# A third buffer for the raw weight chunks of a fused decoder layer

## The chip, the cores and the metric

The kernel runs on one core of a Trainium2 chip. The metric is the device time of one execution in microseconds, taken as the median of several runs. The engines are named as in the profile: PE is the matrix engine, PEld its weight loads, DVE the vector engine, ACT the scalar engine, POOL the general engine GpSimd, and SP the engine that issues most of the DMA transfers.

## The reference

One layer of a decoder for 256 tokens with 1024 features, all in float32: a gated sum of block attention (16 heads of 64; with 256 tokens there is one block, so it is plain causal attention) and a gated linear recurrence (8 heads), then cross-attention to 256 memory tokens (4 heads of 256), then a SwiGLU feed-forward part with 2816 hidden features.

```python
xn = rmsnorm(h, norm_mix_g[l])
q_a, k_a, v_a, q_b, f_b, i_b, og_b, g_a, g_b = split_cols(xn @ w_in[l])
y_a = moba_attention(q_a, k_a, v_a, positions) @ w_br_attn[l]
y_b = hgrn2(q_b, f_b, i_b, og_b, lb_all[l], hgrn_norm_g[l]) @ w_br_hgrn[l]
merged = jax.nn.sigmoid(g_a) * y_a + jax.nn.sigmoid(g_b) * y_b
h = h + merged @ w_out[l]
h = h + memory_cross_attention(rmsnorm(h, norm_x_g[l]), rmsnorm(mem, norm_mem_g[l]),
                               wq_x[l], wkv_x[l], wo_x[l])
hn = rmsnorm(h, norm_ffn_g[l])
gu = hn @ w_ffn_in[l]
h = h + (jax.nn.silu(gu[..., :FFN_HIDDEN]) * gu[..., FFN_HIDDEN:]) @ w_ffn_out[l]
return rmsnorm(h, final_norm_g)
```

## The kernel before, in words

All weights are laid out in main memory as chunks of 1 MB (128 partitions x 2048 floats), in the order in which they are used. Chunks 0 to 63 belong to the part ahead of the feed-forward part: 0 to 35 are the nine input projections, 36 to 47 the two branch projections and the output projection `w_out`, 48 to 59 the cross-attention's keys, values and queries, 60 to 63 its output projection. Each matrix product is made from three products of reduced-precision operands: every number is split into a rounded part `hi` and a remainder `lo`.

So each chunk takes three steps. SP issues its load into a buffer `raw` (L204; the first chunks in pieces at L202 and L208). ACT copies it in two halves to `hi` (L210), and DVE subtracts to get `lo` (L214); for chunks 9 to 41 POOL takes a part of the subtraction. Then PE multiplies. This is the function `prep`; `nxt` calls it so that chunk i+2 is prepared in the program when chunk i is about to be used. `raw` has two buffers in turn (chunk 1 alone has another place), `hi` and `lo` three each. A load waits until the chunk that had the buffer before is converted; a conversion waits until PE is done with the chunk that had the `hi` buffer three chunks before. The chunks 62 and 63 have places of their own for `hi` and `lo` (called `hix` and `lox` in the profile), where the cross-attention's keys and queries were.

The order of PE's instructions is the program's. In the part ahead of the feed-forward part the order on ACT, DVE and SP, and on POOL but for the opening, is made by a planner: it lays out the instructions by its own costs, program order giving the priority, and each engine then runs its list in order, waiting where an operand isn't there. In the feed-forward part all orders are the program's.

Small work runs between the chunks: `tick`, called after each chunk, advances generators for the recurrence (`hgrn`), the causal attention (`attention`, two heads at a time in `duo`: scores L805, maxima L812, exponentials L817, scaling L821, transposes L829, value products L838) and the cross-attention (`scores`: maxima L1046, xmx L1048, exponentials L1050, scaling L1054, transposes L1060). For the fourth cross-attention head the scores come after chunk 58, the transposes after chunk 59, and then `pv` multiplies by the values `vxh` and `vxl` (L319, L320 from `ev_vx`).

Other memory that matters: `H` holds the input by token (x, 1 MB, L540), loaded in the opening; its squares give the norm r_x (L560), from which the first gates `fth` (L512) are made. H is next used at the output projection, where the residual is added (`add_h`). `QQ` (place B6, 16 KB per partition) holds the recurrence's query variants for two groups of four heads; the same place holds later `oal`, `qxl`, `lox` and then the feed-forward's `hids`. QK (place P0) holds the recurrence's queries and keys. In the background ACT and POOL issue transfers from main memory to main memory that make sums of feed-forward weights (`sum`, L228, L232, L234).

Of the kernel before, what the change touches and what calls it, by code (L numbers as in the profile page):

```python
# [11 lines left out]
F32R = mybir.dt.float32r  # L12
I32 = mybir.dt.int32
AF = mybir.ActivationFunctionType
# [15 lines left out]
TOKENS = ((0, 1), (1, 2), (2, 4), (4, 8))  # L30
WARM = 15
PIECES = (4, 2, 2)

D1, D2, D3, D4 = 6434.0, -0.01824188232421875, -3.5660341382026672e-06, 2.549093241608853e-10
C1, C2, C3 = 6.28125, 0.0019354820251464844, -1.748455600074497e-07
# [98 lines left out]
def build(tc, A, out):  # L134
    nc = tc.nc
    V, SC, G, PE, SY = nc.vector, nc.scalar, nc.gpsimd, nc.tensor, nc.sync
    with ExitStack() as ctx:
# [11 lines left out]
        def big(tag, name, shape=(128, 8, 256), dt=F32):  # L149
            return bp.tile(list(shape), dt, name=name, tag=tag)  # L150
# [21 lines left out]
        ifq, posi = gv[:, 56:88], gv[:, 88:90].bitcast(I32)  # L172
        nhalf = cp.tile([128, 4], F32, name="nhalf")
        ident = cst[:, C_ID:C_ID + 128]
        H = big("B0", "H", (128, 2, 1024))
        ones = cp.tile([128, 1], F32, name="ones")
        V.memset(nhalf, -0.5)
        V.memset(ones, 1.0)
# [5 lines left out]
        def prep(tags=None, raw=None):  # L184
            i = made[0]
            made[0] += 1
            first = i < 2
            if raw is None:
                raw = wr.tile([128, 2048], F32, name="raw", tag="raw")
            assert i in HEAD  # L190
            if tags is None:
                hi = wh.tile([128, 2048], F32R, name="hi", tag="hi")
                lo = wl.tile([128, 2048], F32R, name="lo", tag="lo")
            else:
                hi = big(tags[0], "hix", (128, 2048), F32R)
                lo = big(tags[1], "lox", (128, 2048), F32R)
            pieces = 4 if first else 2
            n = 2048 // pieces
            sent = PIECES[i] if i < len(PIECES) else 1
            for c in range(sent if 0 < i < len(PIECES) else 0):  # L200
                a = slice(c * 2048 // sent, (c + 1) * 2048 // sent)
                SY.dma_start(raw[:, a], piece(A["w"][i], a))  # L202
            if sent == 1:
                SY.dma_start(raw, A["w"][i])  # L204
            for c in range(pieces):
                a = slice(c * n, (c + 1) * n)
                if i == 0:
                    SY.dma_start(raw[:, a], piece(A["w"][i], a))  # L208
                    yield
                SC.activation(hi[:, a], raw[:, a], AF.Copy)  # L210
                cut = (c + 1) * n - (POOL_COLS // pieces if i in SHARED else 0)
                for eng, b in ((V, slice(c * n, cut)), (G, slice(cut, (c + 1) * n))):
                    if b.start < b.stop:
                        eng.tensor_tensor(lo[:, b], raw[:, b], hi[:, b].bitcast(F32), op=ALU.subtract)  # L214
            ready[i] = (hi, lo)
# [85 lines left out]
        def gemm_t(X, evict, between=()):  # L301
            between = list(between)
            pss = [mm.tile([128, 512], F32, name="pst", tag="mm") for _ in range(2)]
            for kh in range(2):
                w = by_k(nxt(), 4)
                for t in range(2):
                    t_part(pss[t], w, X, t, kh)
                    if between:
                        between.pop(0)()
                    if kh == 1:  # L310
                        evict(t, pss[t])
                tick()
# [9 lines left out]
        def rstd_of(ssq, name, n=2, mult=1.0 / D, eps=EPS):  # L322
            v = small("v_", [n])
            V.tensor_scalar(v, ssq, mult, eps, op0=ALU.mult, op1=ALU.add)
            r = cp.tile([128, n], F32, name="r_" + name)
            G.tensor_tensor(r, v, nhalf[:, :n], op=ALU.pow)
            return r
# [142 lines left out]


        fT = big("B4", "fT", (128, 16, 128))
        QK = big("P0", "QK", (128, 2, 16, 128))
        QP, KS = QK[:, 0], QK[:, 1]
        QQ = big("B6", "QQ", (128, 16, 256))

        gate_a = cp.tile([128, 8], F32, name="gate_a")
        gate_b = cp.tile([128, 8], F32, name="gate_b")
# [38 lines left out]
        def ev_q(c):  # L517
            th = {}

            def use(h0, bk):  # L520
                a = slice(2 * h0, 2 * h0 + 4)
                q4 = bk.rearrange(v4, a=2)
                V.tensor_tensor(QP[:, a], q4, fT[:, a], op=ALU.mult)
                SC.activation(QQ[:, a].rearrange("p a (w j) -> p a w j", w=4)[:, :, 0:4:3],
                              q4.rearrange("p a (j w) -> p a w j", w=2), AF.Copy)

            def ev(t, ps):
                th[t] = t2("qth")
                SC.activation(th[t], ps, AF.Silu, scale=r_x[:, t:t + 1])
                if t == 1:  # L530
                    turned(th, c, use)
            return ev
# [4 lines left out]
        run(prep())  # L537
        SY.dma_start(cst, A["cst"])
        run(prep())
        SY.dma_start(H, A["xtok"])  # L540
        SY.dma_start(lm, A["lm"])
        pss = [[mm.tile([128, 512], F32, name="psg", tag="mm") for _ in range(2)] for _ in range(2)]
        for i in range(9):
            if i < 8:
                c, k = i // 4, i % 4
                for z in (Xh, Xl):
                    for t in range(2):
                        PE.matmul(pss[c][t], z[:, k, t * 128:(t + 1) * 128], ws[c][0][:, k],
                                  start=z is Xh and k == 0, stop=False)
# [4 lines left out]
        w = by_k(nxt(), 4)  # L554
        for t in range(2):
            t_part(pss[0][t], w, X, t, 1)
        ssqx = small("ssqx", [2])
        junk = big("P1", "junk", (128, 2, 1024))
        for t in range(2):
            SC.activation(junk[:, t], H[:, t], AF.Square, accum_out=ssqx[:, t:t + 1])  # L560
        r_x = rstd_of(ssqx, "x")
        next(rt)
        next(rt)
        r_half = cp.tile([128, 2], F32, name="r_half")
# [5 lines left out]
        w = by_k(nxt(), 4)  # L570
# [33 lines left out]
        def level_one(g, bs):  # L604
            for b in bs:
                a0 = 8 * g + 2 * b
                ps = bank("l1", (128, 2, 64))
                for j in range(2):
                    PE.matmul(ps[:, j], KS[:, a0 + j], QQ[:, a0 + j, 0:64], start=True, stop=True)
                V.tensor_tensor(by_parity(a0, 0), ps, bc(ident2[:, :, 0], 2, 1), op=ALU.mult)  # L610

        def widen(g, L, parts="qkt"):
# [23 lines left out]
        def pair_queries(g, L):  # L636
            ga = slice(8 * g, 8 * g + 8)
            n = 32 // L
            mv = [QQ[:, ga, 64 * i:64 * i + 64] for i in range(3)]
            SC.activation(mv[0].rearrange("p a (i j) -> p a i j", j=L), blocks(QP[:, ga], L)[1], AF.Copy)  # L640
            widen(g, L, "qt")
            wide = blocks(QP[:, ga], 2 * L)[1]
            SC.activation(mv[1].rearrange("p a (i j) -> p a i j", j=2 * L), wide, AF.Copy)
            near = tview(L, g).rearrange("p a (i w) -> p a i w", w=4)[:, :, :, 1]
            V.tensor_tensor(mv[2].rearrange("p a (i j) -> p a i j", j=2 * L), wide,
                            near.unsqueeze(3).to_broadcast([128, 8, n, 2 * L]), op=ALU.mult)

        def pair_levels(g, L, bs):
            for b in bs:
                a0 = 8 * g + 2 * b  # L650
                n = 256 if L == 2 else 192
                ps = bank("lp", (128, 2, n))
                for j in range(2):
                    PE.matmul(ps[:, j], KS[:, a0 + j], QQ[:, a0 + j, 0:n], start=True, stop=True)  # L654
                if L == 2:
                    V.tensor_tensor(by_parity(a0, 1), ps[:, :, 192:256], bc(two_rows, 2, 1), op=ALU.mult)
                for i in range(3):
                    M = L if i == 0 else 2 * L
                    li = (1 if L == 2 else 4) + i
                    mask = lm[:, 64 * li:64 * li + 64].rearrange("p (i j) -> p i j", j=M)  # L660
                    V.copy_predicated(blocks(at3[:, a0:a0 + 2], M)[1], bc(mask, 2, 1),
                                      ps[:, :, 64 * i:64 * i + 64].rearrange("p a (i j) -> p a i j", j=M))
# [219 lines left out]
        def ev_g(dst, c):  # L882
            def ev(t, ps):
                SC.activation(dst[:, t, c * 512:(c + 1) * 512], ps, AF.Tanh, scale=r_half[:, t:t + 1])
            return ev
# [23 lines left out]
        turns = []  # L909
        for c in range(2):  # L910
            gemm_t(X, ev_g(tbt, c))
        tat = big("B7", "tat", (128, 2, 1024))
        for c in range(2):
            gemm_t(X, ev_g(tat, c))
# [149 lines left out]
        for c in range(4):  # L1064
            gemm_f(H1, ev_sum(qxh, qxl, c))
            g = scores(c)
# [123 lines left out]
        raws += spare + [big("B12", "raw", (128, 2048))]  # L1190
        fetch(4)
        fetch(5)
        hids = big("B6", "hids", (128, 4, 2, 2, 256), F32R)
        Sh = big("P1", "Sh", (128, 2, 4, 4, 128), F32R)
        ts = {}

# [40 lines left out]
        def turn_hid(o):  # L1237
            bk = four[1].rearrange("p (a b) -> p a b", a=2)
            for t in range(2):
                u = hm.pop((o, t))  # L1240
                for j in range(2):
                    PE.transpose(bk[:, j, t * 128:(t + 1) * 128], u[:, j * 128:(j + 1) * 128], ident)
            hd = hids[:, o % 4]
            hid[o] = hd

            def post():
                split(bk, hd[:, 0], hd[:, 1])
            return post
# [37 lines left out]
        for k, u in enumerate(FFN[:-2]):  # L1286
            if u[0] == "I":
                ahead(k)
                w = use(k)
# [170 lines left out]
```

## Time and profile before

| | |
|---|---|
| median of 3 runs | 624.73 us (623.67 to 625.43) |
| the profiled execution, total | 626.06 us |
| its span, first to last instruction | 624.3 us |
| PE busy | 606.2 us (97%) |
| DVE, ACT, POOL busy | 450.5, 369.2, 210.2 us |
| DMA | 154.70 MB, mean 248 GB/s |
| mean granted clock of PE | 0.991 |

A row of the view of groups or of the timeline names the source line, the engine, the operation, and what it writes and reads ("raw<-w" is a load of a weight chunk). In the timeline the first two columns are start and duration in microseconds; a bracket at the end gives the idle time of the engine before this instruction and what ended it. In the view of waits each row gives who waited, for whom, the total in microseconds, how often, and the longest. In the view by stretches each row has the busy time and the number of instructions of each engine, then the granted clock of PE, the share of the 16 DMA engines that was busy, and GB/s.

### The profile page before, as it was taken

The page shows a single profiled execution, that of the slowest core. Times are in us where ns is not written, and L with a number is a line of the kernel's source. Part 1 is how long each engine was busy: PE and PEld are TensorE (multiplying, and loading weights), DVE is VectorE, ACT ScalarE, POOL GpSimd, SP SyncE. Part 2 cuts the span into 40 slices and gives each one's busy share as a digit, 9 for nine tenths or more (in the row PEclk, how much of TensorE's full clock was granted, in tenths as well). Part 3 has the DMA queues.
Part 4 walks back from the last instruction along what each step waited for, and adds up shares of the span by engine and source line. Part 5 has one row for each costly group of instructions (what it writes and reads, how often), then busy time and mean ns, then how long its engine had stood idle before and what let it go on. Part 6 is the DMA issues. An engine that isn't in the chain of part 4 may idle for free.

```text
span 624.3 us, 8396 instructions
## 1 busy us (share of the span) xinstructions
PE 606.2 (97%) x3075; PEld 503.1 (81%) x3075; DVE 450.5 (72%) x729; ACT 369.2 (59%) x583; POOL 210.2 (34%) x202
## 2 busy tenths in 40 slices
PE   8999999999999999999999999959999999999995
PEld 7888888888877887778888888858888888888884
DVE  7556678987776775747966557746789878787863
ACT  7775454334267666745546557555477767676752
POOL 3887844665464565343302433100000000000003
PEclk9999999999999999999999999979999999999998
DMA  9775898636875656797798887765699989896601
GB/s 342 289 276 210 266 318 262 228 140 198 270 208 204 257 152 198 276 322 265 228 286 240 304 283 239 229 256 203 264 289 356 307 333 288 319 319 227 195 1 67
DMA packets 21689, 154.70 MB, mean 248 GB/s; under 512 B 2720, under 2 KB 3360, under 8 KB 5280
## 3 DMA queue, kind: packets, MB, share of 16 engines
q1 hardware_dynamic: 17568, 116.63, 49.4%
q0 software_dynamic: 2880, 20.97, 17.4%
q10 hardware_dynamic: 1200, 16.57, 7.0%
q8 instruction: 24, 0.39, 0.2%
q14 instruction: 17, 0.14, 0.1%
HBM read 153.11 MB, written 32.51 MB: 297 GB/s over the span
## 4 chain that ended last, share of the span: by engine, by line
PE 78%; DMA 9%; DVE 8%; ACT 2%; issue 1%; POOL 0%; POOLq 0%; ACTq 0%; DVEq 0%; SPq 0%
PE pst L275 10%; PE pst L277 10%; PE pst L276 10%; DMA raw<-w 8%; PE bk L275 6%; PE bk L277 6%; PE bk L276 6%; DVE lo L214 4%; PE psf L290 3%; PE acc L275 3%; PE acc L277 3%; PE acc L276 3%; PE lp L654 2%; PE psf L291 2%; ACT hi L210 1%
## 5 line engine op out<-in xcount | busy, mean ns | idle before, releaser
L214 DVE TENSOR_TENSOR lo<-raw,hi 128x576 fp32r<-128x576 f32 (+2 forms) x128 | 143.7, 1137 | 68.4 <-ACT hi L210 67.4
L210 ACT ACTIVATE hi<-raw 128x1024 fp32r<-128x1024 f32 (+1 forms) x128 | 128.0, 1028 | 109.1 <-DMA raw<-w 53.6
L214 POOL TENSOR_TENSOR lo<-raw,hi 128x448 fp32r<-128x448 f32 x66 | 98.0, 1504 | 79.2 <-ACT hi L210 72.9
L275 PE MATMUL pst<-hi,Xh 128*128 128x512 f32 x256 | 103.2, 403 | 0.0
L277 PE MATMUL pst<-hi,Xl 128*128 128x512 f32 x256 | 99.9, 390 | 0.0
L276 PE MATMUL pst<-lo,Xh 128*128 128x512 f32 x256 | 99.7, 390 | 0.0
L1165 DVE TENSOR_TENSOR lo<-raw,hi 128x1024 fp32r<-128x1024 f32 x56 | 65.9, 1218 | 13.0 <-ACT hi L1164 12.8
L1164 ACT ACTIVATE hi<-raw 128x1024 fp32r<-128x1024 f32 x56 | 56.2, 1053 | 19.8 <-issue 10.5
L277 PEld LDWEIGHTS pst<-hi,Xl 128*128 128x128 f32 x256 | 48.0, 188 | 10.3
L275 PEld LDWEIGHTS pst<-hi,Xh 128*128 128x128 f32 x256 | 48.1, 188 | 10.0 <-issue 0.7
L276 PEld LDWEIGHTS pst<-lo,Xh 128*128 128x128 f32 x256 | 48.2, 188 | 9.2
L1147 POOL DMA_DIRECT2D raw<-w x5 | 4.5, 891 | 119.2 <-DVE lo L1165 29.7
L275 PE MATMUL acc<-hi,hids 128*128 128x512 f32 x64 | 25.1, 392 | 0.0
L277 PE MATMUL acc<-hi,hids 128*128 128x512 f32 x64 | 24.9, 390 | 0.0
L276 PE MATMUL acc<-lo,hids 128*128 128x512 f32 x64 | 24.9, 389 | 0.0
L275 PE MATMUL bk<-hi,Sh 128*128 128x512 f32 x60 | 23.7, 396 | 0.0
L275 PE MATMUL bk<-hi,h2h 128*128 128x512 f32 x60 | 23.7, 394 | 0.0
L277 PE MATMUL bk<-hi,h2l 128*128 128x512 f32 x60 | 23.4, 390 | 0.0
L277 PE MATMUL bk<-hi,Sh 128*128 128x512 f32 x60 | 23.4, 390 | 0.0
L276 PE MATMUL bk<-lo,h2h 128*128 128x512 f32 x60 | 23.4, 389 | 0.0
L276 PE MATMUL bk<-lo,Sh 128*128 128x512 f32 x60 | 23.3, 389 | 0.0
L290 PE MATMUL psf<-H,hi 128*128 128x512 f32 x64 | 22.8, 400 | 0.0
(388 smaller groups left out, 1446.8 us busy)
## 6 DMA issues: line engine op xcount, KB each, us to landing
raw<-w SPq DMA_DIRECT2D x78, 1024.0 KB, 6.4
sum<-w POOLq DMA_DIRECT2D x15, 1024.0 KB, 9.8
raw<-sum SPq DMA_DIRECT2D x13, 1024.0 KB, 6.9
raws<-w SPq DMA_DIRECT2D x11, 1024.0 KB, 6.7
raw<-w POOLq DMA_DIRECT2D x5, 1024.0 KB, 8.7
raw<-w SPq DMA_DIRECT2D x4, 512.0 KB, 6.1
raws<-sum SPq DMA_DIRECT2D x2, 1024.0 KB, 6.3
raw<-w SPq DMA_DIRECT2D x4, 256.0 KB, 4.5
```

The lines of the kernel that those rows point to most:

```text
L210: SC.activation(hi[:, a], raw[:, a], AF.Copy)
L214: eng.tensor_tensor(lo[:, b], raw[:, b], hi[:, b].bitcast(F32), op=ALU.subtract)
L275: PE.matmul(ps, xh, h, start=first, stop=False, skip_group_check=more)
L276: PE.matmul(ps, xh, l, start=False, stop=False, skip_group_check=more)
L277: PE.matmul(ps, xl, h, start=False, stop=last, skip_group_check=more)
L290: PE.matmul(ps, w[0][:, k, a], X2[:, :, k], start=k == 0, stop=False)
L291: PE.matmul(ps[:, 0], w[1][:, k, a], X2[:, 0, k], start=False, stop=k == 7)
L654: PE.matmul(ps[:, j], KS[:, a0 + j], QQ[:, a0 + j, 0:n], start=True, stop=True)
L1147: G.dma_start(raw_of[k], A["w"][AT_CHUNK["I", PAIRS[g][0], 1]], accum_op=ALU.add)
L1164: SC.activation(hi[:, a], raw[:, a], AF.Copy)
L1165: V.tensor_tensor(lo[:, a], raw[:, a], hi[:, a].bitcast(F32), op=ALU.subtract)
```

## The change

Every third raw chunk (2, 5, 8, ...) of the part ahead of the feed-forward part no longer takes one of the two buffers in turn, but a place of its own: up to chunk 29 the place B0, where H was, and from chunk 32 on the place B6b. B6b is the second half of what was B6: QQ becomes two tiles of half the size, one for each group of heads, and `hids` becomes two tiles likewise. B0 is free at the start since the token-major input is first loaded to the place P0 as `xtok`, where its squares are written over it (before, they went to a tile `junk` at P1), and QK takes P0 after it. The input is loaded a second time to H, at B0, in the program after the chunks of the gate g_b. The number of the other instructions is as it was.

```diff
@@ prep
             first = i < 2
-            if raw is None:
+            if raw is None and i % 3 == 2:
+                raw = big("B0" if i < THIRD else "B6b", "raw", (128, 2048))
+            elif raw is None:
                 raw = wr.tile([128, 2048], F32, name="raw", tag="raw")
...
-        QK = big("P0", "QK", (128, 2, 16, 128))
-        QP, KS = QK[:, 0], QK[:, 1]
-        QQ = big("B6", "QQ", (128, 16, 256))
+        xtok = big("P0", "xtok", (128, 2, 1024))
+        QQ = [big(tag, "QQ", (128, 8, 256)) for tag in ("B6", "B6b")]
...
-        SY.dma_start(H, A["xtok"])
+        SY.dma_start(xtok, A["xtok"])
...
-        junk = big("P1", "junk", (128, 2, 1024))
         for t in range(2):
-            SC.activation(junk[:, t], H[:, t], AF.Square, accum_out=ssqx[:, t:t + 1])
+            SC.activation(xtok[:, t], xtok[:, t], AF.Square, accum_out=ssqx[:, t:t + 1])
         r_x = rstd_of(ssqx, "x")
+        QK = big("P0", "QK", (128, 2, 16, 128))
+        QP, KS = QK[:, 0], QK[:, 1]
...
         for c in range(2):
             gemm_t(X, ev_g(tbt, c))
+        H = big("B0", "H", (128, 2, 1024))
+        SY.dma_start(H, A["xtok"])
...
-        hids = big("B6", "hids", (128, 4, 2, 2, 256), F32R)
+        hids = [big(tag, "hids", (128, 2, 2, 2, 256), F32R) for tag in ("B6", "B6b")]
```

THIRD is 32. The rest of the diff only renames the places where QQ and hids are read and written.

More of the change, by code (lines that the diff above doesn't have):

```diff
@@ L32 @@
 PIECES = (4, 2, 2)
+THIRD = 32
 D1, D2, D3, D4 = 6434.0, -0.01824188232421875, -3.5660341382026672e-06, 2.549093241608853e-10
@@ L174, in build @@
         ident = cst[:, C_ID:C_ID + 128]
-        H = big("B0", "H", (128, 2, 1024))
         ones = cp.tile([128, 1], F32, name="ones")
@@ L523, in use @@
                 V.tensor_tensor(QP[:, a], q4, fT[:, a], op=ALU.mult)
-                SC.activation(QQ[:, a].rearrange("p a (w j) -> p a w j", w=4)[:, :, 0:4:3],
+                qa = slice(a.start % 8, a.start % 8 + 4)
+                SC.activation(QQ[a.start // 8][:, qa].rearrange("p a (w j) -> p a w j", w=4)[:, :, 0:4:3],
                               q4.rearrange("p a (j w) -> p a w j", w=2), AF.Copy)
@@ L608, in level_one @@
                 for j in range(2):
-                    PE.matmul(ps[:, j], KS[:, a0 + j], QQ[:, a0 + j, 0:64], start=True, stop=True)
+                    PE.matmul(ps[:, j], KS[:, a0 + j], QQ[g][:, a0 + j - 8 * g, 0:64], start=True, stop=True)
                 V.tensor_tensor(by_parity(a0, 0), ps, bc(ident2[:, :, 0], 2, 1), op=ALU.mult)
@@ L638, in pair_queries @@
             n = 32 // L
-            mv = [QQ[:, ga, 64 * i:64 * i + 64] for i in range(3)]
+            mv = [QQ[g][:, :, 64 * i:64 * i + 64] for i in range(3)]
             SC.activation(mv[0].rearrange("p a (i j) -> p a i j", j=L), blocks(QP[:, ga], L)[1], AF.Copy)
@@ L653, in pair_levels @@
                 for j in range(2):
-                    PE.matmul(ps[:, j], KS[:, a0 + j], QQ[:, a0 + j, 0:n], start=True, stop=True)
+                    PE.matmul(ps[:, j], KS[:, a0 + j], QQ[g][:, a0 + j - 8 * g, 0:n], start=True, stop=True)
                 if L == 2:
@@ L1242, in turn_hid @@
                     PE.transpose(bk[:, j, t * 128:(t + 1) * 128], u[:, j * 128:(j + 1) * 128], ident)
-            hd = hids[:, o % 4]
+            hd = hids[o % 4 // 2][:, o % 2]
             hid[o] = hd
```

## The prediction

> **What bounds the kernel now.** I read the page first: TensorE (PE) is busy nearly all the span, so only its idle time, and any time at a lower granted clock, can be won. Then the waits of PE alone say where it idles.
>
> ```profile
> span 624.3 us, 8396 instructions
> PE 606.2 (97%) x3075; PEld 503.1 (81%) x3075; DVE 450.5 (72%) x729; ACT 369.2 (59%) x583; POOL 210.2 (34%) x202
> PE xT L1060 <- DVE xp L1054: 6.3, 1, 6.3
> PE aT L829 <- DVE ap L821: 1.7, 3, 0.9
> PE warm L365 <- DVE still L362: 1.6, 1, 1.6
> PE xs L277 <- POOL qxl L1017: 0.8, 1, 0.8
> PE as L805 <- ACT pT L831: 0.5, 1, 0.5
> PE psg L548 <- ACT hi L210: 0.4, 1, 0.4
> PE mT L903 <- POOL tat L898: 0.3, 1, 0.3
> ```
>
> PE idles 624.3 - 606.2 = 18.1 us. The seven waits hold 11.6 of it; the other 6.5 belong to no wait of PE's, most of it the tail after the last matmul, which the change doesn't touch. One wait, 6.3 us before the transposes of the fourth cross-attention head (L1060), is over half of what could move. The ACT and DVE queues around it:
>
> ```profile
> 403.13 0.57 ACT L316 ACTIVATE ph<-xT 128x512 fp32r<-128x512 f32 x1
> 409.79 2.00 ACT L210 ACTIVATE hix<-raw 128x1024 fp32r<-128x1024 f32 x2 [6.08 <-DMA raw<-w]
> 411.69 0.58 ACT L1050 ACTIVATE xp<-xp,xmx,r 128x256 f32<-128x256 f32 x1
> 404.75 0.15 DVE L1048 SCALAR_TENSOR_TENSOR xmx<-xmx,r 128x2 f32<-128x2 f32 x1
> 404.81 1.22 DVE L214 TENSOR_TENSOR lo<-raw,hi 128x1024 fp32r<-128x1024 f32 x1
> 413.07 1.20 DVE L214 TENSOR_TENSOR lox<-raw,hix 128x1024 fp32r<-128x1024 f32 x1
> 414.19 0.61 DVE L1054 TENSOR_SCALAR xp<-xp,xsum 128x256 f32<-128x256 f32 x2
> 414.72 1.40 DVE L320 SCALAR_TENSOR_TENSOR vxl<-pst,r_m,vxh 128x512 fp32r<-128x512 f32 x2
> ```
>
> The head's maxima are ready at 404.90, but its exponentials (L1050) start at 411.69: they stand in ACT's queue behind the conversion of chunk 62 (hix), which waits 6.08 us for that chunk's load. PE waits for weights that it doesn't need until much later. The pause also costs clock afterwards (columns: stretch, us, busy time of PE, PEld, DVE, ACT, POOL, granted clock, DMA share, GB/s):
>
> ```profile
> 394.50:400.70 6.20, 6.20 (x32) 5.24 (x32) 4.30 (x9) 3.75 (x8) 2.92 (x3) 1.00 0.42 149
> 408.10:414.60 6.50, 0.17 (x2) 0.01 (x1) 2.84 (x5) 4.32 (x8) 0.00 (x0) 0.78 0.46 166
> 414.60:418.60 4.00, 4.00 (x19) 3.92 (x20) 2.21 (x4) 0.84 (x2) 0.00 (x0) 0.51 0.76 276
> 418.60:422.60 4.00, 4.00 (x35) 4.00 (x35) 3.36 (x4) 3.98 (x5) 0.00 (x0) 1.00 0.59 248
> 160.00:190.00 30.00, 28.80 (x162) 23.19 (x161) 20.66 (x42) 16.56 (x29) 14.20 (x10) 1.00 0.87 280
> ```
>
> At clock 0.51 PE starts 19 matmuls in 4 us, at full clock 35 of the same kind. Four of the 19 are half as wide, so they would have taken (15 + 2) / 35 x 4 = 1.9 us plus about 0.2 for the switch: some 1.9 us lost.
>
> **The change, part by part.**
>
> *The third buffer.* Chunks 57 to 63 now use the two old slots (57, 58, 60, 61, 63) and a third one (59, 62). So chunk i waits for the conversion of chunk i-3, no longer i-2: its load can be issued when that of chunk i-1 was issued before. The 61 loads of L204 are chunks 3 to 63 in order. The issues of chunks 61 and 62, and from the DMA view the times to landing of chunks 59, 60 and 62:
>
> ```profile
> L204 SPq DMA_DIRECT2D raw<-w x61: 327/328/882, 9.7 to 406.1; - x61
> 391.28 0.33 SPq L204 DMA_DIRECT2D raw<-w  x1
> 399.91 0.33 SPq L204 DMA_DIRECT2D raw<-w  x1
> raw<-w SPq DMA_DIRECT2D x1, 1024.0 KB, 4.7
> raw<-w SPq DMA_DIRECT2D x1, 1024.0 KB, 10.7
> raw<-w SPq DMA_DIRECT2D x1, 1024.0 KB, 9.8
> ```
>
> Chunk 62 moves from 399.91 to 391.28. With the longest landing here, 10.7 us, it lands at 402.0, against 409.7; DMA had room, with a share of 0.42 in 394.5 to 400.7. ACT is free for hix when ph ends, 403.70: so hix runs 6.09 us earlier, to 405.7, and the exponentials follow to 406.8. What is late next is DVE: its lo of chunk 61 ends at 406.03, then two lox of 1.2 with a short reciprocal between, and xp starts near 408.5; the transposes came 0.41 us after xp's start (414.19 to 414.60), so at 408.9. PE is free at 414.60 - 6.33 = 408.27: 0.6 us of idle stay. Right after, DVE's two vxl take 1.40 us from about 409.05, to 410.4, while the first value product reaches the matmul that reads the second of them after four transposes and five matmuls, near 409.9: another 0.5 us. Waits of this length cost no clock: the waits of 160 to 190 (0.93 and 0.27 us, below) left it at 1.00. The step gives 6.3 - 0.6 - 0.5 + 1.9 = 7.1 us; bounds 0 (ACT still stands) and 8.2.
>
> The Trainium skill, "TensorE: Matmul & The Clock Gate", section "Why this matters for your kernels", says that a pause of more than about 3 us between bursts puts TensorE at half rate. The 0.51 after 6.33 us agrees. By that rule a remainder of up to 3 us would still save the whole clock loss; by scaling the row, one of 3 us would keep some 0.9 of it.
>
> *The same step in the attention stage.* Two of its three PE waits trace to a load:
>
> ```profile
> 179.40 2.01 ACT L210 ACTIVATE hi<-raw 128x1024 fp32r<-128x1024 f32 x2 [1.64 <-DMA raw<-w]
> 184.38 0.61 PE L829 MATMUL aT<-cst,ap 128*128 128x128 f32 x3 [0.93 <-DVE ap L821]
> 185.26 0.61 PE L829 MATMUL aT<-cst,ap 128*128 128x128 f32 x3 [0.27 <-DVE ap L821]
> 187.83 1.06 ACT L210 ACTIVATE hi<-raw 128x1024 fp32r<-128x1024 f32 x1 [3.24 <-DMA raw<-w]
> 194.18 0.33 PE L829 MATMUL aT<-cst,ap 128*128 128x128 f32 x1 [0.49 <-DVE ap L821]
> 162.50 0.33 SPq L204 DMA_DIRECT2D raw<-w  x1
> 174.48 0.33 SPq L204 DMA_DIRECT2D raw<-w  x1
> ```
>
> The load for the conversion at 179.40 (chunk 28) moves from 174.48 to 162.50; the one for 187.83 moves likewise. With ACT no longer standing 1.64 and 3.24 us, I take 1.4 of the 1.69 us (0.3 stays, DVE's own lo stands between); bounds 0 and 1.7.
>
> *The other five waits.* warm and psg (1.6 and 0.4 us) lie in the opening, before a third buffer matters. xs (0.8) waits for a POOL result that stood behind a conversion in ACT's queue, and that one for PE's release of a hi buffer, which stays; as and mT (0.5, 0.3) wait for evictions. 0, bounds 0 and 1.6 gained.
>
> *Loads that are queued earlier at the start.* Chunk 3 no longer waits, and chunk 4 waits for chunk 0, so it may go ahead of the token-major input in SP's queue, where it stood behind it.
>
> ```profile
> 5.00:20.00 15.00, 14.58 (x64) 11.62 (x64) 14.31 (x30) 11.81 (x21) 8.91 (x12) 1.00 1.03 410
> 25.68 1.25 ACT L512 ACTIVATE fth<-psg,r_half 128x512 f32<-128x512 f32 x2
> 27.68 0.49 PE L490 MATMUL fT__411<-cst,fth 128*128 128x128 f32 x3
> ```
>
> DMA is saturated there, so xtok would land 1.05 MB / 410 GB/s = 2.6 us later, and with it the squares, r_x and the gates (fth). The second gate ends at 26.3, PE needs it at 27.68: 1.4 us of cover, so 0 to 1.2 us lost. ACT's conversion of chunk 4 stands between the two gates now and, loaded earlier, would go ahead of the squares; I take 0.
>
> *The second load of 1 MB* stands in SP's queue behind chunk 33. It needs slot B0 after chunk 29, whose conversion is the one at 187.83, four chunks earlier, and H is first read by the output projection, chunk 44: SP waits for nothing new. The loads behind it lose up to one transfer (4.7 us undisturbed), covered by the extra buffer's period: (406.1 - 9.7) / 60 = 6.6 us per chunk. 0, bounds 0 and 0.5 lost. Splitting QQ and hids, and squaring in place, change no count and no duration: 0.
>
> *The new order.* Outside PE, a planner orders the queues of the first part by its own times, and earlier slots change them. Its price isn't shown before; the nearest rows are the small waits above, 0.3 to 0.9 us each, gained or lost. I take 0 and keep 2 lost for the range.
>
> **Sum.** 7.1 + 1.4 = 8.5 us. The profiled execution took 626.1 us, 1.8 more than its span, and would take 617.6; it is 1.3 above the runs' median, 624.7, from which I forecast 616.2. Everything after 422 us only moves earlier: PE has no wait in it.
>
> **Rivals.**
>
> *Another load takes the place.* If the planner also puts chunk 63's conversion ahead of the exponentials, ACT waits for a load that is issued when chunk 60 is converted, at 399.91. With a landing of 9.8 us and 2.0 of conversion the exponentials start at 411.7, as now: 624.7 - 1.4 = 623.3. With one of 4.7 they start at 406.6, 0.9 after the forecast's: 617.1. Against it: the maxima are ready 1.2 us after hix can start, so the head, earlier in the program, should come next.
>
> *The load is issued earlier but shares the engines.* Two weight loads beside the sums' transfers, each at half rate: 62 takes 2 x 9.8 from 391.28, landing 410.9, 1.2 later than now: 624.7 - 1.4 + 1.2 = 624.5, no change. Against it stands the free share of 0.42. The Trainium skill, "DMA: Bandwidth & Descriptors", section "Issuing engines are not separate DMA queues", says that transfers of all issuing engines run on the same 16 DMA engines and interleave, which is this rival's ground; 4.7 us for one landing and 10.7 for the next, in the rows above, agrees.
>
> *Slower: conversions in front of softmax.*
>
> ```profile
> ACT hi L210 <- DMA raw<-w: 53.6, 21, 11.8
> ACT hi L210 <- PE pst L277: 43.7, 16, 4.7
> ```
>
> Data that comes earlier lets the planner put a conversion ahead of a head's exponentials while PE still holds its hi buffer. ACT then waits 43.7 / 16 = 2.7 us; at 184 its 1.64 us became 1.2 us of PE, so 2.0 each. There are eight head pairs and four cross-attention heads. From six such places it decides: 616.2 + 12 = 628.2. Against it: ACT has 16 such waits now, and of PE's seven only xs, 0.8 us, traces to one.
>
> **Chances.** Forecast 0.72 (from 613.2, where all waits but those of opening and tail go: 624.7 - 9.6 - 1.9, to 619.4, with 1.2 lost at the start and 2 in the order); the other load 0.10; sharing 0.09; slower 0.09. A measurement tells about 0.3%, 1.9 us, from no change: faster is the forecast and most of the other load, 0.81; same 0.10, slower 0.09. The range 613.2 to 623.3 takes in the first two cases, 0.82; the forecast alone has 613.2 to 619.4.
>
> **What would show it.** In the profile after: the wait of xT L1060 at 1 us or less, hix without a DMA wait before it, no stretch near clock 0.5 in the middle, ACT's idle time on raw well under 53.6 us, aT waits under 0.5. I'm wrong if xT still waits over 3 us, or new PE waits of over 2 us in sum appear.

## The result and the profile after

The median fell from 624.34 us (4 runs) to 614.61 us (4 runs): a ratio of 0.985, 95% interval 0.982 to 0.988. The forecast was 616.2, with a range of 613.2 to 623.3. The profiled execution took 617.14 us, the longest of the four, for a reason in the opening that is told below; the other three took 614.4 to 614.7.

The page of the changed kernel; its third line here is the chain of work that ended last, by engine:

```profile
span 615.4 us, 8395 instructions
PE 605.8 (98%) x3075; PEld 503.3 (82%) x3075; DVE 451.1 (73%) x729; ACT 369.8 (60%) x583; POOL 205.8 (33%) x202
PE 92%; DVE 4%; issue 1%; ACT 1%; DMA 1%; POOL 0%; POOLq 0%; DVEq 0%; ACTq 0%
```

The same chain in the kernel before:

```profile
PE 78%; DMA 9%; DVE 8%; ACT 2%; issue 1%; POOL 0%; POOLq 0%; ACTq 0%; DVEq 0%; SPq 0%
```

The waits of PE in the changed kernel (total, times, longest):

```profile
PE warm L367 <- DVE still L364: 1.6, 1, 1.6
PE psg L550 <- ACT hi L212: 0.6, 1, 0.6
PE as L808 <- ACT pT L834: 0.5, 1, 0.5
PE mT L906 <- POOL tat L901: 0.3, 1, 0.3
PE xT L1065 <- DVE xp L1059: 0.2, 1, 0.2
```

The wait before the fourth head's transposes went from 6.3 to 0.2 us; the aT waits (1.7) and the xs wait (0.8) are not in this execution. PE's share of the chain that ended last went from 78% to 92%, and DMA's from 9% to 1%. PE's busy time, 606.2 before, hardly moved in this profile, because it holds a slow opening (below); in a second profile of the same kernel it is 603.6 us.

ACT's timeline at the place of the old wait:

```profile
401.54 1.04 ACT L212 ACTIVATE hix<-raw 128x1024 fp32r<-128x1024 f32 x1
402.49 0.58 ACT L318 ACTIVATE ph<-xT 128x512 fp32r<-128x512 f32 x1
402.97 1.05 ACT L212 ACTIVATE hix<-raw 128x1024 fp32r<-128x1024 f32 x1
403.94 0.60 ACT L1055 ACTIVATE xp<-xp,xmx,r 128x256 f32<-128x256 f32 x1
407.76 2.01 ACT L212 ACTIVATE hix<-raw 128x1024 fp32r<-128x1024 f32 x2 [1.97 <-DMA raw<-w]
```

SP's issue of the loads of chunks 62 and 63, and from the DMA view their times to landing:

```profile
389.86 0.33 SPq L206 DMA_DIRECT2D raw<-w  x1
397.29 0.33 SPq L206 DMA_DIRECT2D raw<-w  x1
```

```profile
raw<-w SPq DMA_DIRECT2D x1, 1024.0 KB, 5.9
raw<-w SPq DMA_DIRECT2D x1, 1024.0 KB, 10.4
```

Chunk 62 is issued at 389.86, not 399.91, and lands at 395.8, almost 6 us before ACT comes to it. Its two conversions still stand ahead of the exponentials, but no longer wait. Chunk 63's conversion does wait for its load, 1.97 us, and the second vxh stands behind it. That costs PE nothing (below).

What the pause cost in clock can be read from two pairs of rows of PE's timeline, the transposes and the same value product 15 instructions later; first the kernel before, then the changed one:

```profile
414.60 1.16 PE L1060 MATMUL xT<-cst,xp 128*128 128x128 f32 x4 [6.33 <-DVE xp L1054]
418.33 0.36 PE L271 MATMUL xo<-pl,vxh 128*128 128x256 f32 x1
```

```profile
407.09 0.81 PE L1065 MATMUL xT<-cst,xp 128*128 128x128 f32 x4 [0.21 <-DVE xp L1059]
409.28 0.28 PE L273 MATMUL xo<-pl,vxh 128*128 128x256 f32 x1
```

3.73 us became 2.19: 1.5 us for the same work.

**The opening of the profiled execution.** The first rows of PE's products, stretch 5 to 11 us, in this profile and in a second profile of the unedited changed kernel (columns as in the prediction):

```profile
5.00:11.00 6.00, 5.40 (x13) 4.14 (x13) 5.50 (x11) 5.27 (x11) 0.62 (x1) 1.00 1.05 408
```

```profile
5.00:11.00 6.00, 6.00 (x26) 4.63 (x26) 5.64 (x10) 5.36 (x11) 0.84 (x2) 1.00 1.05 407
```

13 products against 26 in the same 6 us, with the granted clock shown as 1.00 in both. So the first profile holds a slow opening, in which the first 12 products lose about 2.4 us, and the second doesn't; the second span is 613.3 us, and the four times of that run are 614.2 to 615.1. The comparison of spans, 624.3 to 615.4, understates the change by some 2 us.

### The profile page after: what moved, and what is told of

Read it like the earlier page. It is cut to its first block, busy times and chain, and to the rows that moved or that the text cites. A ratio compares the mean times of both kernels' runs of the same rounds, so it can differ in the third digit from the quotient of the medians.

```text
span 615.4 us, 8395 instructions
## 1 busy us (share of the span) xinstructions
PE 605.8 (98%) x3075; PEld 503.3 (82%) x3075; DVE 451.1 (73%) x729; ACT 369.8 (60%) x583; POOL 205.8 (33%) x202
## 4 chain that ended last, share of the span: by engine, by line
PE 92%; DVE 4%; issue 1%; ACT 1%; DMA 1%; POOL 0%; POOLq 0%; DVEq 0%; ACTq 0%
PE pst L277 13%; PE pst L279 13%; PE pst L278 13%; PE bk L279 6%; PE bk L277 6%; PE bk L278 6%; PE psf L292 5%; PE acc L277 3%; PE acc L278 3%; PE acc L279 3%; PE psf L293 2%; PE lp L657 2%; PE psg L550 2%; DVE lo L216 1%; PE pso L279 1%; PE pso L277 1%
## 5 line engine op out<-in xcount | busy, mean ns | idle before, releaser
L216 DVE TENSOR_TENSOR lo<-raw,hi 128x576 fp32r<-128x576 f32 (+2 forms) x128 | 146.9, 1160 | 54.4 <-ACT hi L212 54.2
L216 POOL TENSOR_TENSOR lo<-raw,hi 128x448 fp32r<-128x448 f32 x66 | 95.8, 1467 | 82.4 <-ACT hi L212 80.5
L1169 ACT ACTIVATE hi<-raw 128x1024 fp32r<-128x1024 f32 x56 | 56.3, 1054 | 20.5 <-issue 10.4
L279 PEld LDWEIGHTS pst<-hi,Xl 128*128 128x128 f32 x256 | 48.0, 188 | 10.4
```

Of the source, the lines that this page charges most:

```text
L279: PE.matmul(ps, xl, h, start=False, stop=last, skip_group_check=more)
```

## The experiments

The theories. **A**: the gain is that chunk 62's load no longer keeps ACT, and so the exponentials behind it, waiting; what else the third buffer does is small. **B**: the planner's new order of the whole first part makes the gain. **C** (called D in one expectation below): all loads being earlier makes it.

**The third buffer late only, and early only.** H stays at B0 in the first of the two; in the second, chunks from 32 on have two buffers.

```diff
# late only
-            if raw is None and i % 3 == 2:
+            if raw is None and i % 3 == 2 and i >= THIRD:
# early only
+            if raw is None and i % 3 == 2 and i < THIRD:
```

> Third buffer (B6b) for chunks 32, 35, ..., 62 alone; H stays at B0 and is loaded once, as before. Theory A (the gain is that the loads of the cross-attention's last chunks are issued one place earlier, so ACT no longer stands at chunk 62): the two PE waits of that stage, 6.3 and 0.8 us, go, and with them up to 1.9 us of slow clock; the three aT waits (1.7 us) stay. 624.3 - 7.1 - (0 to 1.9) = 615.3 to 617.2. Theory B (the gain is the planner's new order of the whole first part): without the early change its order differs, and the gain is not predictable, anywhere from 616 to 624. Theory C (freed room in the queues early on matters most): above 621.

> Third buffer (B0) for chunks 2, 5, ..., 29 alone, with xtok and the second load of the input; from chunk 32 on two buffers as before. Theory A: only the aT waits go (1.7 us), the 6.3 us wait of the fourth head's transposes stays: 622.6, and 622 to 624. Theory C: below 619.

Late only: 616.49 us, ratio 0.989 (0.987 to 0.991). Early only: 622.39, ratio 0.998 (0.9965 to 1.0002). Both as A says. PE's waits, late only (one row) and early only (one row):

```profile
PE aT L833 <- DVE ap L825: 1.8, 3, 1.1
```

```profile
PE xT L1065 <- DVE xp L1059: 5.0, 1, 5.0
```

Each half removes its own waits and leaves the other's. C falls.

**One chunk.** Only chunk 62 has the third place, and the input is loaded once, as before; chunk 63 takes the buffer that chunk 62 leaves, and QQ and hids stay in halves.

```diff
+            if raw is None and i == 62:
+                raw = big("B6b", "raw", (128, 2048))
```

> One chunk alone, 62, has the place B6b; all others as before, H loaded once. Theory A: chunk 62 is issued right behind chunk 61 (391.3 in the trace of before instead of 399.9), lands before ACT comes to it, and the 6.3 us wait goes to 0.2 as in the changed kernel, with the clock loss; the xs wait (0.8) and the aT waits (1.7) stay: 624.3 - 6.1 - (0 to 1.9) = 616.3 to 618.2. If one chunk isn't enough (the loads before it must be early too), above 620.

614.99 us, ratio 0.987 (0.985 to 0.989), better than expected: the xT wait fell to 0.4 us as A says, but the aT and xs waits, expected to stay, weren't there either.

```profile
PE as L809 <- ACT pT L835: 0.5, 1, 0.5
PE xT L1064 <- DVE xp L1058: 0.4, 1, 0.4
PE mT L907 <- POOL tat L902: 0.3, 1, 0.3
PE xo L275 <- DVE vxl L323: 0.2, 1, 0.2
```

One thing is not as expected: chunk 62's load was not issued right behind chunk 61's. Its place is free from the moment that PE is done with the second half of QQ, and the planner's list of SP has the load there, some 260 us before it is needed:

```profile
135.03 0.33 SPq L207 DMA_DIRECT2D raw<-w  x1
```

So this run shows that chunk 62's load alone decides over the wait, but not how late the load may be; the changed kernel, which issues it at 389.86, shows that this is early enough.

**The order alone.** The kernel before, with two buffers; the conversions of chunks 62 and 63 are queued on ACT behind the last vxh.

```diff
-                run(prep(tags))
+                with tc.issue_after(last_scaled[0].ins):
+                    run(prep(tags))
```

> The kernel before with its two buffers; the conversions of chunks 62 and 63 are only queued on ACT behind the last vxh (the value copies of the cross-attention), so that the fourth head's exponentials no longer stand behind a conversion that waits for its load. Theory A's mechanism is a queue, not a lack of bandwidth: the 6.3 us wait goes without any third buffer, 616.3 to 618.2 as with one chunk. If PE needed the weights of chunk 62 themselves soon after, a wait moves to the first products of chunk 62 (hix then ends near 412, PE comes to it some 12 us after the transposes): above 620.

> The kernel before with hix queued behind the last vxh, again, beside the changed kernel. Theory A: both lose the same 6.3 us wait and its clock, so the medians lie within 1 us of each other; this one, with two buffers, has the wider spread, since its aT and xs waits (0 to 2.5 us) depend on how long the loads beside the sums take, and the changed kernel's don't.

614.10 us, ratio 0.986 (0.984 to 0.989), and 614.88 the second time, 0.987 (0.985 to 0.990); the changed kernel, run beside the second, 614.77, 0.986 (0.984 to 0.989). So the wait goes without any third buffer. PE's waits, and below them ACT's row of the first half of hix:

```profile
PE warm L366 <- DVE still L363: 1.6, 1, 1.6
PE as L806 <- ACT pT L832: 0.5, 1, 0.5
PE mT L904 <- POOL tat L899: 0.3, 1, 0.3
```

```profile
405.38 1.06 ACT L211 ACTIVATE hix<-raw 128x1024 fp32r<-128x1024 f32 x1
```

hix runs at 405.38, after everything that PE waits for, and no wait for chunk 62's products appears. This shows that the cure needs neither a buffer nor bandwidth: one conversion stood first in an engine's list. The planner's lists of ACT, DVE and POOL in this kernel, in the one with chunk 62 alone and in the late-only one are those of the kernel before up to the fourth head's scores, so the new order of what comes before them doesn't make the gain. Against the rest of B stands the experiment with the last sum below: there the lists of ACT, DVE and SP are those of the kernel before from start to end, and the wait is gone all the same.

**All but chunk 62.** The changed kernel, with chunk 62 back in the two buffers.

```diff
+            if raw is None and i % 3 == 2 and i < 62:
```

> The changed kernel, but chunk 62 goes back to the two buffers in turn, so it waits for chunk 60's conversion as before the change; all other chunks keep the third buffer. Theory A: the big wait comes back nearly whole: ACT's list has both halves of hix ahead of the exponentials, the load is issued near 397 to 399 and lands 9 to 10 us later: 5 to 6.3 us of PE wait and up to 1.9 us of slow clock more than the changed kernel, 620 to 622.5. Theory D (the gain comes from all loads being early): below 617.

621.86 us, ratio 0.9977 (0.9963 to 0.9992). ACT stands again, and PE with it:

```profile
405.18 2.00 ACT L212 ACTIVATE hix<-raw 128x1024 fp32r<-128x1024 f32 x2 [5.41 <-DMA raw<-w]
```

PE's wait for it:

```profile
PE xT L1065 <- DVE xp L1059: 5.5, 1, 5.5
```

All the other earlier loads together are worth 1.4 us (0.0023 x 623.7; 0.5 to 2.3), chunk 62's the rest.

**The two loads and the moves, without the buffer.**

```diff
-            if raw is None and i % 3 == 2:
-                raw = big("B0" if i < THIRD else "B6b", "raw", (128, 2048))
-            elif raw is None:
+            if raw is None:
                 raw = wr.tile([128, 2048], F32, name="raw", tag="raw")
```

> Everything of the change but the third buffer: xtok at P0, its second load to H at B0 (which SP issues early, since B0 is empty), QQ and hids in halves, two raw buffers. Theory A: the second load and the moves cost nothing, PE's 6.3 us wait stays: as the kernel before, within 0.3%. If the second load costs: up to 1 us slower.

623.84 us, ratio 1.0004 (0.998 to 1.002): they cost nothing that can be told.

**The transfer beside it.** The kernel before; the last background sum is moved into the feed-forward part.

```diff
-            if i >= 4 and (i - 4) * 6 // 11 != (i - 3) * 6 // 11:
+            if 4 <= i < 58 and (i - 4) * 6 // 11 != (i - 3) * 6 // 11:
...
+            if k == 2:
+                G.dma_start(summed[-1][2], A["w"][AT_CHUNK["I", PAIRS[-1][1], 1]], accum_op=ALU.add,
+                            max_dma_last_dim=8192)
```

> The kernel before, two buffers and its order; only the last of the background sums (POOL's accumulate transfer of 1 MB that is issued at 398.75, 1.2 us ahead of chunk 62's load) is moved into the feed-forward part. Theory A with sharing of the DMA engines as the reason that chunk 62's load took 9.8 us: it lands in 4.7 to 6.7 us, so ACT stands 1 to 3 us instead of 6.1, PE's wait before xT falls to 1.3 to 3.3 us, and the clock loss goes below 3 us: 618 to 621. If the transfer beside it doesn't matter, no change: 623.6.

616.77 us, ratio 0.991 (0.988 to 0.993): a third cure, and more than expected. Two of its six times, 619.1 and 620.7, are longer than the rest (615.5 to 617.7); the profile is not of one of these, so what they waited for is open. Chunk 62's load in the DMA view, and below it PE's waits:

```profile
raw<-w SPq DMA_DIRECT2D x1, 1024.0 KB, 4.8
```

```profile
PE aT L829 <- DVE ap L821: 1.2, 2, 0.9
PE bk L275 <- DVE fc L1282: 0.9, 1, 0.9
PE xT L1060 <- DVE xp L1054: 0.2, 1, 0.2
```

The load takes 4.8 us without that transfer. In the six profiles of kernels that leave both the load and the transfer where they were, it takes 9.7 to 10.2. ACT no longer stands at all; I had priced a landing of up to 6.7. The wait of 0.9 us at bk, in the feed-forward part, is in no other profile; the moved transfer is the likely cause, but this was not tested.

**Buffer and order together, and a longer warm-up.**

> The changed kernel with the order of the experiment on order added: hix of chunks 62 and 63 on ACT behind the last vxh. Theory A: the big wait is gone by either, so they don't add up: the time of the order alone, 614.1, less what the early third buffer saves of the aT and xs waits where they appear (0 to 2.5 us in one execution): 612.5 to 614.6. If they were two independent gains: below 608.

> Third buffer and order together, and 18 instead of 15 warm-up matmuls in the opening, so that PE doesn't pause between them and the first products. If the pause of 0.1 to 0.6 us decides at times whether the clock rises before 7 us or near 11, the median stays at 613.7 to 614.3 and no execution lies above 615; if the rise has nothing to do with it, there are executions near 616 as before; three more matmuls of 0.24 us at half clock could delay the first product by up to 0.5 us.

> The changed kernel again, unedited, beside the next two, for its spread and its rank. In its first profile the opening's first 12 matmuls (5.7 to 11.0 us) stood 0.425 us apart instead of 0.23, some 2.4 us lost, after a pause of 0.60 us behind the warm-up matmuls. If the change causes that, the profile shows it again; if it depends on the execution, the spacing reaches 0.23 by about 7 us as in the other kernels' profiles, the span is 612.5 to 613.5, and the time 614.0 to 615.0.

Both: 613.99 us, ratio 0.985 (0.983 to 0.987). They don't add up, since they remove the same wait. With 18 warm-up matmuls besides: 614.53 (614.2 to 614.6), 0.986 (0.983 to 0.988), beside the changed kernel's 614.77; no difference that can be told, and since the changed kernel, run beside it, showed no slow opening either, whether the pause after the warm-up causes it stays open. The version with both is the lowest measured, but not told apart from the changed kernel. In one thing they differ from the order alone: eight executions of "both" and "both, longer warm-up" span 613.8 to 614.6, ten of the order alone, with two buffers, 613.7 to 616.7. The changed kernel's own eight span 614.2 to 617.1, the longest being the one with the slow opening.

## Why the prediction was right, point by point

**The third buffer at chunk 62.** Right in mechanism and size: 7.1 us expected (6.3 less 1.1, and 1.9 of clock), 6.1 plus 1.5 = 7.6 measured in the traces, 8.1 by the kernel with chunk 62 alone (0.013 x 623.6), which in its profile has also lost the aT and xs waits. Three terms of it were off. The 0.6 us that should stay before the transposes was 0.2: as I had it, DVE's list sets the time, but in the changed kernel its two lox begin 2.5 us before PE is free (404.36 and 406.88), not 2.2, and take 2.3 us to xp, not 2.5. The 0.5 us for vxl was wrong in kind: chunks 58 and 59 supply the values of the third and fourth head, while the first value product reads the first head's. So chunk 63's conversion, which the rival rightly put ahead of something, stands before a vxh that isn't needed yet: this rival came half true. It cost PE nothing in the changed kernel and 0.2 us in the one with chunk 62 alone (its row for xo above). And the clock's 1.9 us, 1.5 in this pair of profiles, is not one number. In the three other profiles that have the pause (early only, two loads, all but 62) PE's slow stretch lasted 3.3, 3.1 and 6.0 us, against 3.9 before. From the first transpose to the output projection's first product these four took 7.7 to 8.9 us, against 6.4 in the second profile of the changed kernel: 1.3 to 2.5 us lost. The slow stretch of all but 62 in the view by stretches:

```profile
409.99:415.90 5.91, 5.91 (x28) 5.83 (x29) 3.48 (x6) 2.74 (x4) 0.00 (x0) 0.50 0.82 323
```

**Sharing.** The rival's ground is real: without the transfer beside it the same load took 4.8 us. It failed because the earlier issue, at 389.86, took chunk 62's load out of the way of that transfer, which POOL issues at 396.13 in the changed kernel; there it is chunk 63's load, issued at 397.29, that takes 10.4 us.

**The attention stage.** 1.4 us expected; all earlier loads but chunk 62's measured 1.4 (0.5 to 2.3). That is little for ACT's idle time before hi that is put down to loads, which fell from 53.6 to 2.6 us: nearly all of it had cost PE nothing. That 1.4 was expected and 1.4 measured is luck: I took the three aT waits of one profile as a property of the kernel, but some executions have them and others don't. In the profiles without the early third buffer they go with the time to landing of chunk 24's load, which is issued at 139 to 140 us beside a background sum:

| kernel | landing of chunk 24's load, us | PE's aT waits, us |
|---|---|---|
| before | 10.9 | 1.7 |
| late only | 10.9 | 1.8 |
| last sum later | 11.0 | 1.2 |
| chunk 62 alone | 9.8 | none |
| order alone | 9.5 | none |
| order alone, again | 9.6 | none |
| two loads, no buffer | 9.4 | none |

Four of these, the kernel before, the last sum later and both of the order alone, have the same lists and buffers up to there, two with the waits and two without. So one us more or less in one landing goes with 1.2 to 1.8 us of PE. That is an observation over seven executions; no kernel took that transfer alone away. The step was right in kind: the six profiles with the early third buffer have no aT wait, though in four of them the load beside the same sum took 10.9 to 11.0 us. A profile of the kernel before is thus a sample. Its 23 times beside the second group of experiments span 621.1 to 626.1 us, those of the kernel with all but chunk 62 changed 620.9 to 623.0. But the early buffer alone doesn't narrow the spread (620.8 to 626.5 over 12 executions), so the aT waits are not all of it; the clock after the pause varies too.

**The wait of xs**, said to stay: it went, also in kernels with two buffers. The conversion ahead of it in the kernel before:

```profile
374.82 1.06 ACT L210 ACTIVATE hi<-raw 128x1024 fp32r<-128x1024 f32 x1 [3.23 <-PE psf L290]
```

Its load's issue on SP, and the time to landing:

```profile
367.25 0.33 SPq L204 DMA_DIRECT2D raw<-w  x1
```

```profile
raw<-w SPq DMA_DIRECT2D x1, 1024.0 KB, 7.5
```

The bracket names PE, but the load landed at 367.25 + 7.5 = 374.7, 0.1 us before the conversion began. I had read the bracket and not the landing. In the order alone the same load took as long, 7.6 us, but was issued 12.1 us before PE's first xs product (362.66 and 374.80), here 10.3 (367.25 and 377.58), and the wait is gone; why its issue came earlier there stays open.

**The start.** xtok did land later, by 2.6 us as expected in the first profile (the squares begin at 22.28, before at 19.70) and by 3.8 us in the second (23.52). In the first profile the slow opening hid it; in the second, with the opening fast, PE waits 0.38 + 0.25 us for the gates, inside the bounds of 0 to 1.2 and not the 0 I took:

```profile
27.76 0.33 PE L491 MATMUL fT__411<-cst,fth 128*128 128x128 f32 x1 [0.38 <-ACT fth L513]
28.34 0.33 PE L491 MATMUL fT__411<-cst,fth 128*128 128x128 f32 x1 [0.25 <-ACT fth L513]
```

**The second load, the moves, the order.** 0 expected; 1.0004 measured for the loads and moves. No new wait of the planner's making shows in the changed kernel, and the slower rival didn't come.

**The sum.** 8.5 us expected, 9.7 measured by the medians, with an interval of 7.4 to 11.1. By the profiles, the first step gave 0.4 and 0.5 more and 0.4 less for the clock, the attention stage 0.3 more, xs 0.8 more, and the start cost 0.6: 1.0 in all. That the sum comes so close to the 1.2 is in part luck, since aT, xs and the clock's share differ from one execution to the next; the wait at chunk 62 is in all four profiles that keep its late load, its transfer and its place in the list.

## What to carry to other kernels

When a busy engine waits for a result, look at what stands ahead of it in the list of the engine that makes the result: here a conversion of weights that were needed much later stood first and waited for its load. Three cures gave nearly the same time, an earlier load (a buffer), a later place in the list (no memory at all), or less traffic beside the load; so a wait for a load doesn't yet say that a buffer is missing, and the cheapest cure here is the order. And take a wait of a microsecond or two in one profile as a sample: check against a second execution, and check what a bracket names against the landing time, before pricing its removal.

## What the runs showed of the hardware

Chunk 62's load of 1 MB took 4.8 us when the transfer beside it, which accumulates 1 MB in main memory, was moved away, and 9.7 to 10.2 us with it. In the 13 profiles all loads of raw that SP issued 0.4 to 1.6 us behind POOL's issue of such a transfer took 8.4 to 11.4 us, those issued less than 0.1 us behind it 4.6 to 5.4 us. That the same load, chunk 24's, differs by 1.5 us from one execution to the next (9.5 and 11.0 us) was not expected. After a pause of 5.0 to 6.3 us the products of 256 columns started 0.21 us apart instead of 0.12, for 3.1 to 6.0 us; the granted clock of the profile shows it (0.50 to 0.51 in four profiles). The length doesn't go with that of the pause: the longest pause, 6.3 us, was followed by 3.9 us, one of 5.5 us by 6.0. In the opening of one execution of the changed kernel the products of 512 columns stood 0.425 us apart instead of 0.23 for 5 us, and there the clock column reads 1.00. The spacing tells it, the clock column alone doesn't.
